# Gate products of a gated linear recurrence: three rounded-fp32 products of high and low halves in place of plain fp32

## The chip, the cores and the metric

The kernel runs on one core of one Trainium2 chip. The metric is the device time of one execution in microseconds (us), and of several executions the median. The core has five engines that work side by side, each with a queue of its own: TensorE (PE) multiplies matrices, VectorE (DVE) and GpSimd (POOL) do elementwise work, ScalarE (ACT) does functions of one input, and SyncE (SP) issues transfers.

## What is computed

One step of a decoder layer for a prompt of 2048 tokens and 8 single tokens of other sequences, all in fp32. After an RMSNorm one combined projection gives five parts. Two of them feed a gated linear recurrence (RG-LRU) of width 512, three feed an attention over a sliding window of 128 tokens. Both results are normalised, put side by side, projected back, and a feed-forward part (SwiGLU, 1024 to 2816 to 1024) follows. The change concerns the two gates of the recurrence, `r` and `i`:

```python
xc, new_conv = _causal_conv(xr, conv_buf, conv_w, conv_b)      # width 4
xb = xc.reshape(xc.shape[:-1] + (8, 64))                       # 8 blocks of 64
r = sigmoid(einsum('btni,nij->btnj', xb, gate_a_w) + gate_a_b)
i = sigmoid(einsum('btni,nij->btnj', xb, gate_x_w) + gate_x_b)
log_a = -8.0 * r * softplus(-lru_lambda)
a = exp(log_a)
u = sqrt(-expm1(2.0 * log_a)) * (i * xc)
h = scan(h * a + u)                                            # over the tokens
rec = h * gelu(gr)
```

## The kernel before

Channels lie on the 128 partitions and tokens on the columns. The 2056 tokens are cut into four sub-blocks: sub-block 0 has 520 columns (the 8 single tokens are its last 8) and is multiplied as two pieces of 260; sub-blocks 1 to 3 have 512. For each of them the input projection runs as 14 units of 128 output channels (`ip<s>_<u>` in the order of matmuls, `ip` in the profile), then come the recurrence, the attention (`s`, `pt`, `o`), and the output projection (`op`). Tokens of all sub-blocks then go through the feed-forward part, which fills the time from 679 us on.

A product of two fp32 matrices is made of rounded fp32 (F32R): each operand is split into a high half, its rounding, and a low half, what the rounding left; `mm3` (L423) issues high times high, high times low and low times high into one accumulator. Weights are split on the way in: `split_raw` has ScalarE round 128x512 values (L368) and GpSimd subtract (L369), and in `w_in0_3_1` the names mean unit 3, second half of the rows, first sub-block (later sub-blocks load the split weights back).

The recurrence runs in `rec_chunk(s, c)` (L768) for each sub-block `s` and each chunk `c` of 128 of the 512 channels: 16 times. GpSimd keeps the last three columns of the chunk in `hist`; the convolution makes `xc` by one operation of ScalarE (L781) and three of VectorE (L786); then come the gates, for each of which a block-diagonal 128x128 matrix is multiplied with `xc` in **plain fp32** (L796 to L802): one matmul per piece of columns, so 4 in sub-block 0 and 2 in the others per chunk, 40 in all (16 of 260 columns, 24 of 512). Their names are `g<s>_<c>_<gate>_<first column>`. ScalarE takes the tanh of each straight from PSUM into `ra` or `ia` (L802). The gate weights stand in one tile `gw`, 128x1024, that SyncE loads in `prologue` (L624).

Order: TensorE's is written out by hand in `PE_ORDER` (L112) up to the start of the feed-forward part; a key with `:n` stands for the next n matmuls of that name, and a key that begins with `w_` for fillers that multiply ones while something else is awaited (`filled`, L311). `order_pe` (L414) chains them, so that a matmul that waits holds all behind it. The other engines' order is chosen when the program is built: a scheduler simulates the engines and takes the ready instruction of the best priority; priorities are due times that the generators of the stages (`Chains`, L234) yield, and `AFTER` (L106) pins seven pairs. So a new instruction on one engine can change the order on all of them. The gate products take turns in one PSUM tile (`ps_m`, one buffer) with other short ones.

```python
for gi, (dst, hb) in enumerate(((ra, hab), (ia, hxb))):
    for n0, nn in nbl:
        ps = m_tile(f"g{s}_{c}_{gi}_{n0}")
        with ahead():
            mm(f"g{s}_{c}_{gi}_{n0}", ps[:, :nn], gw[:, (gi * 4 + c) * P:(gi * 4 + c + 1) * P], xc[:, n0:n0 + nn],
                             start=True, stop=True)
        nc.scalar.activation(dst[:, n0:n0 + nn], ps[:, :nn], AF.Tanh, bias=hb[:, c:c + 1], scale=0.5)
```

Of the kernel before, what the change touches and what calls it, by code (L numbers as in the profile page):

```python
# [117 lines left out]
ip0_8_1:4 bc_x0_4 ip0_8_1:20 ip0_0_0:24 ip0_0_1:23 g0_1_0_0 ip0_0_1 ip0_3_0:24 g0_1_0_260 ip0_3_1:17 g0_1_1_0  # L118
ip0_3_1:7 ip0_11_0:18 g0_1_1_260 ip0_11_0:6 ip0_11_1:15 vt0_0 ip0_11_1:9 ip0_10_0:23 vt0_1 ip0_10_0 ip0_10_1:24
ip0_13_0:10 vt0_2 ip0_13_0:14 ip0_13_1:6 vt0_3 ip0_13_1:18 ip0_2_0:7 s0_0_0:4 ip0_2_0:5 g0_0_0_0 s0_0_1:4 ip0_2_0:12  # L120
ip0_2_1:6 s0_1_0:4 s0_1_1:4 ip0_2_1:2 g0_0_0_260 ip0_2_1:13 pt0_0_1:4 ip0_2_1 s1_0_0:4 ip0_2_1:2 ip0_5_0:3 s1_0_1:4
ip0_5_0 g0_0_1_0 ip0_5_0:9 o0_0_0 ip0_5_0:11 ip0_5_1 s1_1_0:4 ip0_5_1:2 pt0_1_1:4 o0_0_0 ip0_5_1:4 g0_0_1_260
ip0_5_1:12 s1_1_1:2 o0_1_0 s1_1_1:2 ip0_5_1:5 ip0_4_0:6 s2_0_0:4 ip0_4_0:3 o0_1_0 ip0_4_0:11 pt1_0_0:4 ip0_4_0:2
s2_0_1:4 ip0_4_0:2 ip0_4_1:24 ip1_8_0:15 ip0_6_0:2 o1_0_0 ip0_6_0:8 pt1_0_1 o1_0_0 pt1_0_1:3 ip0_6_0 ip1_8_0
g0_3_0_0 ip0_6_0:13 ip0_6_1 ip1_8_0:2 ip0_6_1:15 o1_0_1 g0_3_0_260 s2_1_0:4 ip0_6_1 ip1_8_0 ip0_6_1 pt1_1_0
ip0_6_1:5 o1_0_1 s2_1_1:4 pt1_1_0:3 ip0_6_1 ip1_8_0:5 ip1_9_0 g0_3_1_0 ip1_9_0:19 ip0_7_0:9 ip1_9_0:2 pt1_1_1 o1_1_0
pt1_1_1:3 g0_3_1_260 ip1_9_0:2 ip0_7_0:2 o1_1_0 ip0_7_0:13 w_bc_x1_0 bc_x1_0 s3_0_0:3 s3_0_1:4 ip0_7_1 s3_0_0
ip0_7_1 o1_1_1:2 bc_x1_0 w_pt2_0_0:4 ip0_7_1 bc_x1_0 ip0_7_1 bc_x1_0 ip0_7_1:2 pt2_0_0:4 ip0_7_1:18 ip1_10_0:2
o2_0_0:2 pt2_0_1:3 g0_2_0_0 ip1_10_0:12 pt2_0_1 ip1_10_0:10 ip1_11_0:2 o2_0_1 ip1_11_0 s3_1_0:4 pt2_1_0:4 g0_2_0_260
# [158 lines left out]
def hybrid_step(tc, xT, xR, vecs, cst, gatew, win, wout, wgate, wup, wdown, kT, vC, ck, cv, sconv, sh0,  # L288
# [4 lines left out]
    with ExitStack() as ctx:  # L293
# [291 lines left out]
        with ExitStack() as actx:  # L585
# [3 lines left out]
            ap2 = A(tc.tile_pool(name="ap2", bufs=2))  # L589
            ap3 = A(tc.tile_pool(name="ap3", bufs=2))  # L590

            gw = ap1.tile([P, 1024], F32, name="gw")
            hist = ap1.tile([P, CR, 3], F32, name="hist")
            nc.vector.memset(hist, 0.0)
            carry = ap1.tile([P, CR], F32, name="carry")
# [1134 lines left out]
```

## Time and profile before

| | us |
|---|---|
| median of 3 runs | 2060.22 |
| lowest and highest | 2058.54, 2064.38 |
| the profiled execution: its span | 2054.6 |
| the profiled execution: its own time | not given apart from the span |

One execution was taken by the hardware profiler. Its span is the time from the first to the last instruction of the engines; "busy" is the sum of the records of an engine. A group row names the line, the engine, the operation, the result and its operands, then shapes and types, the count, and behind the bar busy us, mean ns of one, and the idle time of the engine just ahead of these instructions with what ended it. A row of the timeline has the start in us, the duration in us, engine, line, operation, operands and the count of instructions joined, and in brackets the idle time ahead of it and what ended that. A stretch has its bounds and length, the busy time of TensorE's matmuls, of its weight loads, of VectorE, ScalarE and GpSimd with their counts, the granted clock of TensorE, and the share and rate of the transfers. The engine PEld is the weight load, which overlaps the matmuls. A matmul's record reaches to the modelled end of its pipeline, so records of neighbours overlap. L396 is the line of the helper through which all matmuls pass; one plain fp32 matmul leaves two records.

### The profile page before, as it was taken

How to read it: one execution, taken by the hardware profiler on the slowest of the kernel's cores; microseconds unless marked ns; L12 is line 12 of the kernel's file. 1: busy time of each engine (PE TensorE's matmuls, PEld its weight loads, DVE VectorE, ACT ScalarE, POOL GpSimd, SP SyncE). 2: the span in 40 equal slices, each digit the busy share in tenths (PEclk: the TensorE clock that was granted, in tenths of full speed). 3: DMA queues.
4: the chain of work that ended last, by engine and by line, in shares of the span. 5: the costliest groups of instructions: out<-in, count | busy, mean ns of one | idle time of the engine just before them, and what ended most of it. 6: DMA issues, size and time to landing. Idle time of an engine off the chain costs nothing.

```text
span 2054.6 us, 34857 instructions
## 1 busy us (share of the span) xinstructions
PE 2015.9 (98%) x12319; PEld 1908.1 (93%) x12319; DVE 1459.9 (71%) x2694; ACT 944.6 (46%) x1960; POOL 906.5 (44%) x799
## 2 busy tenths in 40 slices
PE   9999999999999999999999999999999999999998
PEld 9988787878777899999999999999999999999998
DVE  6877886767985766666654667777768666777675
ACT  6764774553664543343334533333335433433343
POOL 5311342020122787567656645556457522322333
PEclk9999999999999999999999999999999999999999
DMA  9864584576688856666546677776677675566652
GB/s 329 293 213 143 188 275 159 175 233 210 208 261 280 314 200 223 205 210 207 207 172 210 229 260 258 227 229 221 222 253 265 211 251 189 183 197 196 197 179 96
DMA packets 208991, 450.98 MB, mean 219 GB/s; under 512 B 25232, under 2 KB 82720, under 8 KB 208800
## 3 DMA queue, kind: packets, MB, share of 16 engines
q1 hardware_dynamic: 205184, 445.73, 65.2%
q10 hardware_dynamic: 3632, 3.02, 0.4%
q8 instruction: 97, 1.59, 0.3%
q14 instruction: 78, 0.64, 0.1%
HBM read 335.89 MB, written 113.84 MB: 219 GB/s over the span
## 4 chain that ended last, share of the span: by engine, by line
PE 77%; DVE 9%; DMA 6%; ACT 3%; issue 2%; POOL 1%; SPq 0%; DVEq 0%; ACTq 0%; POOLq 0%
PE ps_u L396 19%; PE ps_g L396 19%; PE pw L396 11%; PE pd L396 10%; PE ip L396 10%; PE op L396 4%; DMA n<-hs 3%; DMA xs<-in_xT 1%; DMA m<-mixed 1%; PE o L396 1%; PE pt L401 1%; DVE sc L974 1%; DVE sc L963 1%; PE s L396 1%; DMA mixed<-n 1%
## 5 line engine op out<-in xcount | busy, mean ns | idle before, releaser
L396 PE MATMUL ps_g<-hn,w_g 128*128 128x342 f32 (+1 forms) x2772 | 489.4, 320 | 4.6 <-DVE c_u L1410 1.8
L396 PE MATMUL ps_u<-hn,w_u 128*128 128x342 f32 (+1 forms) x2772 | 479.9, 319 | 1.9 <-ACT c_u L1436 1.3
L396 PEld LDWEIGHTS ps_g<-hn,w_g 128*128 128x128 f32 x2772 | 445.1, 188 | 6.0 <-DVE c_u L1410 2.3
L396 PEld LDWEIGHTS ps_u<-hn,w_u 128*128 128x128 f32 x2772 | 444.2, 188 | 2.6 <-ACT c_u L1436 1.6
L396 PE MATMUL ip<-xn,w_in 128*128 128x512 f32 (+1 forms) x1680 | 353.4, 358 | 1.9 <-ACT xn L431 1.8
L396 PEld LDWEIGHTS ip<-xn,w_in 128*128 128x128 f32 x1680 | 270.1, 189 | 46.0 <-issue 3.8
L1500 DVE TENSOR_TENSOR y<-y,pw 128x342 f32<-128x342 f32 x504 | 238.7, 504 | 73.0 <-PE pw L396 72.2
L396 PE MATMUL pd<-fh,w_d 128*128 128x344 f32 (+1 forms) x960 | 239.4, 320 | 0.6 <-DVE y L1469 0.6
L396 PE MATMUL op<-mix,w_out 128*128 128x512 f32 (+1 forms) x960 | 203.4, 357 | 0.5 <-DVE rrec L763 0.3
L396 PEld LDWEIGHTS op<-mix,w_out 128*128 128x128 f32 x960 | 155.4, 188 | 29.3 <-issue 5.0
L1469 DVE TENSOR_TENSOR y<-y,pd 128x344 f32<-128x344 f32 (+1 forms) x240 | 117.9, 507 | 75.3 <-PE pd L396 70.7
L396 PEld LDWEIGHTS pd<-fh,w_d 128*128 128x128 f32 x960 | 168.3, 188 | 1.4 <-DVE y L1469 1.1
L396 PE MATMUL pw<-fh,wd 128*128 128x342 f32 x576 | 165.6, 319 | 1.2 <-DVE y L1500 1.2
L396 PE MATMUL pd<-fl,w_d 128*128 128x344 f32 (+1 forms) x480 | 153.4, 320 | 0.0
L1381 DVE TENSOR_TENSOR fl<-c_u,fh 128x342 fp32r<-128x342 f32 (+1 forms) x132 | 107.1, 815 | 48.3 <-ACT fh L1380 47.9
L1225 POOL TENSOR_TENSOR w_u<-ru,w_u 128x512 fp32r<-128x512 f32 x44 | 58.9, 1338 | 181.6 <-ACT w_u L1224 155.0
L1392 POOL TENSOR_TENSOR c_u<-c_u,c_g 128x342 f32<-128x342 f32 (+1 forms) x60 | 60.5, 1008 | 170.7 <-DVE c_u L1410 132.1
L1380 ACT CAST fh<-c_u 128x342 fp32r<-128x342 f32 (+1 forms) x132 | 63.0, 480 | 157.8 <-POOL c_u L1392 61.9
L396 PE MATMUL pw<-t,wd 128*128 128x342 f32 x648 | 126.7, 320 | 2.6 <-DVE t L1381 1.7
L1410 DVE TENSOR_TENSOR c_u<-c_u,ps_u 128x342 f32<-128x342 f32 (+1 forms) x99 | 50.2, 507 | 100.3 <-PE ps_u L396 100.1
L396 PEld LDWEIGHTS pw<-t,wd 128*128 128x128 f32 x648 | 106.0, 188 | 4.4 <-DVE t L1381 2.5
L396 PEld LDWEIGHTS pw<-fh,wd 128*128 128x128 f32 x576 | 105.3, 189 | 1.7 <-DVE y L1500 1.5
(316 smaller groups left out, 3507.4 us busy)
## 6 DMA issues: line engine op xcount, KB each, us to landing
w_g<-split_g SPq DMA_DIRECT2D x88, 512.0 KB, 4.2
w_u<-split_u SPq DMA_DIRECT2D x88, 512.0 KB, 4.9
w_in<-split_w SPq DMA_DIRECT2D x84, 512.0 KB, 3.5
rg<-in_wgate SPq DMA_DIRECT2D x110, 256.0 KB, 3.1
ru<-in_wup SPq DMA_DIRECT2D x110, 256.0 KB, 3.2
w_out<-split_w SPq DMA_DIRECT2D x48, 512.0 KB, 4.4
split_g<-w_g SPq DMA_DIRECT2D x44, 512.0 KB, 3.6
split_u<-w_u SPq DMA_DIRECT2D x44, 512.0 KB, 2.7
```

The source lines that it names most:

```text
L396: r = nc.tensor.matmul(*args, **kw)
L401: r = nc.tensor.transpose(*args)
L963: seen[f"sm{gb}_{kv}_{g}"] = nc.vector.tensor_tensor_reduce(sc[:, g, :kn], ps[:, gi * 256:gi * 256 + kn], mask[:, k0:k0 + kn], -SCALE, ns[ ...
L974: nc.vector.tensor_scalar(sc[:, g, :kn], sc[:, g, :kn], mx[:, 1, g:g + 1], None, ALU.mult)
L1225: lo_eng.tensor_tensor(w[:, 1, :], src, w[:, 0, :].bitcast(F32), op=ALU.subtract)
L1380: nc.scalar.copy(hi, v)
L1381: nc.vector.tensor_tensor(lo, v, hi.bitcast(F32), ALU.subtract)
L1392: (nc.vector if p == NPAIR - 1 or src is not v else eng(E_MUL[2 * h + n])).tensor_tensor(v, src, g, op=ALU.mult)
L1410: nc.vector.tensor_tensor(o, a, b, op)
L1469: r = nc.vector.tensor_tensor(ys[gi, n, m], ys[gi, n, m], ps, ALU.add)
L1500: nc.vector.tensor_tensor(v, v, ps, ALU.add)
```

## The change

The gate weights become two rounded tiles: the raw weights are loaded into a buffer of the pool `bigp`, ScalarE rounds them into `gwh`, GpSimd subtracts into `gwl`. Per chunk two new tiles of one buffer each, `xch` and `xcl` (128x520), are filled in the same way from `xc`. Each gate product becomes three rounded ones, `gwh` with `xch`, `gwl` with `xch`, `gwh` with `xcl`: 120 matmuls for 40. In `PE_ORDER` each `g` key has `:3`, and some stand some matmuls later than before. The scratch for dynamic DMA is set to 2 KB when the program object is made.

```diff
-ip0_8_1:4 bc_x0_4 ip0_8_1:20 ip0_0_0:24 ip0_0_1:23 g0_1_0_0 ip0_0_1 ip0_3_0:24 g0_1_0_260 ip0_3_1:17 g0_1_1_0
+ip0_8_1:4 bc_x0_4 ip0_8_1:20 ip0_0_0:24 ip0_0_1:23 ip0_0_1 ip0_3_0:15 g0_1_0_0:3 ip0_3_0:9 g0_1_0_260:3 ip0_3_1:17
...
-            gw = ap1.tile([P, 1024], F32, name="gw")
+            gwh = ap1.tile([P, 1024], F32R, name="gwh")
+            gwl = ap1.tile([P, 1024], F32R, name="gwl")
...
-                keep(nc.sync.dma_start(gw, gatew))
+                raw = bigp.tile([P, 2 * TM], F32, tag="big", name="graw")[:, :1024]
+                keep(nc.sync.dma_start(raw, gatew))
+                nc.scalar.copy(gwh, raw)
+                nc.gpsimd.tensor_tensor(gwl, raw, gwh.bitcast(F32), op=ALU.subtract)
                 keep(nc.sync.dma_start(sh, sh0))
...
+                xh = ap1.tile([P, TM], F32R, tag="xch", name=f"xch{s}_{c}")
+                xl = ap1.tile([P, TM], F32R, tag="xcl", name=f"xcl{s}_{c}")
+                nc.scalar.copy(xh[:, :T], xc[:, :T])
+                nc.gpsimd.tensor_tensor(xl[:, :T], xc[:, :T], xh[:, :T].bitcast(F32), op=ALU.subtract)
                 yield (t + D_REC[0], "prologue")
...
                         ps = m_tile(f"g{s}_{c}_{gi}_{n0}")
+                        cols = slice((gi * 4 + c) * P, (gi * 4 + c + 1) * P)
                         with ahead():
-                            mm(f"g{s}_{c}_{gi}_{n0}", ps[:, :nn], gw[:, (gi * 4 + c) * P:(gi * 4 + c + 1) * P], xc[:, n0:n0 + nn],
-                                             start=True, stop=True)
+                            for i, (w, x) in enumerate(((gwh, xh), (gwl, xh), (gwh, xl))):
+                                mm(f"g{s}_{c}_{gi}_{n0}", ps[:, :nn], w[:, cols], x[:, n0:n0 + nn], start=i == 0, stop=i == 2)
...
-    nc = bacc.Bacc("TRN2", target_bir_lowering=False, num_devices=1)
+    nc = bacc.Bacc("TRN2", target_bir_lowering=False, num_devices=1, dynamic_dma_scratch_size=2048)
```

What the rows below show is an engine's instructions in the order in which it runs them: line, operation, result and operands (each name with a running number behind it), shape, and how many alike. On GpSimd, early in sub-block 0, where the weights of units 0, 3 and 11 are split and the chunk 1 of the recurrence has its `xc`, this stood before:

```order
L369 TENSOR_TENSOR w_in0_0_1_514<-raw_in0_0_1_512,w_in0_0_1_514 128x512
L902 COPY kvn_152<-kraw0_153 128x8
L369 TENSOR_TENSOR w_in0_3_0_596<-raw_in0_3_0_594,w_in0_3_0_596 128x512
L369 TENSOR_TENSOR w_in0_3_1_602<-raw_in0_3_1_600,w_in0_3_1_602 128x512
L773 COPY xr0_3_592<-hist_133 128x3
L777 COPY hist_133<-xr0_0_504 128x3
L369 TENSOR_TENSOR w_in0_11_0_690<-raw_in0_11_0_688,w_in0_11_0_690 128x512
```

and this stands there now:

```order
L369 TENSOR_TENSOR w_in0_0_1_522<-raw_in0_0_1_520,w_in0_0_1_522 128x512
L931 COPY kvn_153<-vraw0_155 128x8
L911 COPY kvn_153<-kraw0_154 128x8
L369 TENSOR_TENSOR w_in0_3_0_612<-raw_in0_3_0_610,w_in0_3_0_612 128x512
L800 TENSOR_TENSOR xcl0_1_445<-xc0_1_435,xch0_1_444 128x520
L777 COPY xr0_3_608<-hist_134 128x3
L369 TENSOR_TENSOR w_in0_3_1_618<-raw_in0_3_1_616,w_in0_3_1_618 128x512
L781 COPY hist_134<-xr0_0_512 128x3
L369 TENSOR_TENSOR w_in0_11_0_706<-raw_in0_11_0_704,w_in0_11_0_706 128x512
```

The new subtraction of `xcl0_1` and the copy into `xr0_3` have come ahead of the second half of the weights of unit 3, and the order of `hist` and `kvn` has changed. On ScalarE, during the output projection of sub-block 0 (`xt3_1` and `xt3_2` are sums for the norm over loaded rows of sub-block 3, `pth5_1_1` is the rounded transposed probabilities of attention block 5), this stood before:

```order
L741 ACTIVATE xt3_0_4179,xsums3_161<-xt3_0_4179 128x512
L802 ACTIVATE ia1_2_2990<-g1_2_1_0_2999,hxb_150 128x512
L814 ACTIVATE q21_1_3005<-a1_2_3004 128x512
L368 CAST w_out0_6_0_3449<-raw_out0_6_0_3447 128x512
L442 ACTIVATE sq_h0_3_3435<-xres0_3_3237 128x520
L781 ACTIVATE xc1_3_3036<-xr1_3_2828,vec_99 128x512
L741 ACTIVATE xt3_2_4368,xsums3_161<-xt3_2_4368 128x512
L984 CAST pth5_1_1_2457<-pt5_1_1_2452 128x512
L741 ACTIVATE xt3_1_4262,xsums3_161<-xt3_1_4262 128x512
L970 ACTIVATE sc6_1_2511,mx6_1_2512<-sc6_1_2511,mx6_1_2512 128x257 x2
```

and this stands there now:

```order
L368 CAST w_out0_5_1_3460<-raw_out0_5_1_3458 128x512
L811 ACTIVATE ia1_2_3062<-g1_2_1_0_3073,hxb_151 128x512
L368 CAST w_out0_6_0_3533<-raw_out0_6_0_3531 128x512
L745 ACTIVATE xt3_0_4279,xsums3_162<-xt3_0_4279 128x512
L785 ACTIVATE xc1_3_3112<-xr1_3_2892,vec_99 128x512
L442 ACTIVATE sq_h0_3_3519<-xres0_3_3321 128x520
L993 CAST pth5_1_1_2513<-pt5_1_1_2508 128x512
L745 ACTIVATE xt3_1_4366,xsums3_162<-xt3_1_4366 128x512
L979 ACTIVATE sc6_1_2567,mx6_1_2568<-sc6_1_2567,mx6_1_2568 128x257 x2
```

`pth5_1_1` has come ahead of `xt3_2`, which now stands behind these rows. On TensorE, a little ahead of that place (chunk 2 of sub-block 1; the product with `ones` is a filler), this stood before:

```order
L396 MATMUL op0_3_0_3312<-mix0_0_2229,w_out0_3_0_3227 128x260
L396 MATMUL g1_2_0_0_2991<-ones_102 128x256 x5
L396 MATMUL g1_2_0_0_2991<-xc1_2_2885,gw_132 128x512
L401 MATMUL pt5_1_0_2443<-cs_101,sc5_1_2417 128x128
L396 MATMUL op0_3_0_3312<-mix0_0_2229,w_out0_3_0_3227 128x260 x2
L396 MATMUL op0_3_0_3312<-mix0_1_2237,w_out0_3_0_3227 128x260 x3
L396 MATMUL op0_3_0_3312<-mix0_2_2241,w_out0_3_0_3227 128x260 x3
L396 MATMUL op0_3_0_3312<-mix0_3_2603,w_out0_3_0_3227 128x260 x3
```

and this stands there now:

```order
L396 MATMUL op0_3_0_3396<-mix0_0_2285,w_out0_3_0_3311 128x260
L396 MATMUL g1_2_0_0_3063<-ones_102 128x256 x5
L401 MATMUL pt5_1_0_2499<-cs_101,sc5_1_2473 128x128
L396 MATMUL op0_3_0_3396<-mix0_0_2285,w_out0_3_0_3311 128x260 x2
L396 MATMUL op0_3_0_3396<-mix0_1_2293,w_out0_3_0_3311 128x260 x3
L396 MATMUL op0_3_0_3396<-mix0_2_2297,w_out0_3_0_3311 128x260 x2
L396 MATMUL g1_2_0_0_3063<-xch1_2_2958,gwh_132 128x512
L396 MATMUL g1_2_0_0_3063<-xch1_2_2958,gwl_133 128x512
L396 MATMUL g1_2_0_0_3063<-xcl1_2_2959,gwh_132 128x512
L396 MATMUL op0_3_0_3396<-mix0_2_2297,w_out0_3_0_3311 128x260
```

The gate product has moved behind the transposition `pt5_1_0` and seven matmuls of `op0_3_0`; the five fillers have kept their place.

130 lines of the change are left out of this document (65 added, 65 removed).

## The prediction

> **What bounds the kernel now.** I read the page's first part, then the groups of TensorE by shape, then the stretches of 20 us, and last the rows in order of time around the gate products.
>
> ```profile
> span 2054.6 us, 34857 instructions
> PE 2015.9 (98%) x12319; PEld 1908.1 (93%) x12319; DVE 1459.9 (71%) x2694; ACT 944.6 (46%) x1960; POOL 906.5 (44%) x799
> ```
>
> TensorE is busy for all but 38.7 us of the span, so a microsecond taken from its queue is a microsecond of the end, unless another engine then arrives last. The shown runs have a median of 2060.22 us; the profile gives no separate time for its own execution, so I take 5.6 us (2060.2 - 2054.6) as what lies around the span, and every difference below is added to 2060.2.
>
> All gate products lie ahead of 590 us, and in that part there are places where the vector side has no room left (first the tile view of the gate weights, with shortest, median and longest record in ns; then the stretches):
>
> ```profile
> L396 PE MATMUL g<-xc,gw x80: 380/591/697, 40.2 to 589.3; 128*128 128x512 f32 x48, 128*128 128x260 f32 x32
> ...
> 240.00:260.00 20.00, 19.05 (x139) 17.18 (x139) 17.73 (x34) 18.21 (x33) 9.60 (x9) 1.00 0.84 280
> 260.00:280.00 20.00, 16.59 (x125) 15.20 (x124) 18.89 (x32) 16.36 (x37) 12.56 (x12) 1.00 0.93 307
> 480.00:500.00 20.00, 20.00 (x98) 16.27 (x97) 11.12 (x25) 5.23 (x14) 0.19 (x1) 1.00 0.73 235
> 540.00:560.00 20.00, 19.89 (x91) 15.43 (x89) 19.62 (x44) 14.94 (x29) 0.93 (x3) 1.00 0.67 208
> 560.00:580.00 20.00, 19.02 (x86) 14.96 (x87) 19.35 (x38) 13.38 (x26) 3.27 (x4) 1.00 0.77 241
> ```
>
> Columns of a stretch: its bounds, length, busy PE, PEld, DVE, ACT, POOL, granted clock, DMA share, GB/s. At 480 to 500 DVE has 8.9 us free and TensorE alone sets the pace. At 260 to 280 and 540 to 580 DVE is 94 to 98% busy: there a shorter TensorE queue only waits longer.
>
> **TensorE's part.** The tempting rows are the groups:
>
> ```profile
> L396 PE MATMUL g<-xc,gw 128*128 128x512 f32 x48 | 25.1, 605 | 2.5 <-ACT ra L802 2.0 <-DVE xc L786 0.3 <-ACT rb_rc L470 0.2
> L396 PE MATMUL g<-xc,gw 128*128 128x260 f32 x32 | 9.8, 388 | 0.0
> L396 PE MATMUL ip<-xn,w_in 128*128 128x512 f32 x1008 | 263.2, 403 | 0.0
> L396 PE MATMUL ip<-xn,w_in 128*128 128x260 f32 x672 | 92.1, 289 | 1.9 <-ACT xn L431 1.8
> ```
>
> Each plain fp32 product is two records (48 for 24 products of 512 columns, 32 for 16 of 260). By busy time a 512-column product costs 25.1/24 = 1.05 us and three rounded ones 3 x 263.2/1008 = 0.78 us; that would save 24 x 0.26 + 16 x 0.20 = 9.5 us. But busy time counts the pipeline's tail, which the next matmul covers. What the queue pays is from start to start:
>
> ```profile
> 46.20 0.60 PE L396 MATMUL g<-xc,gw 128*128 128x260 f32 x2
> 46.45 3.35 PE L396 MATMUL ip<-xn,w_in 128*128 128x260 f32 x25
> 49.63 0.60 PE L396 MATMUL g<-xc,gw 128*128 128x260 f32 x2
> 49.88 2.87 PE L396 MATMUL ip<-xn,w_in 128*128 128x260 f32 x21
> 52.58 0.27 PE L401 MATMUL vt<-cs,vraw 128*128 128x128 f32 x1
> ...
> 581.77 2.94 PE L396 MATMUL op<-mix,w_out 128*128 128x512 f32 x12
> 584.54 1.02 PE L396 MATMUL g<-xc,gw 128*128 128x512 f32 x2
> 585.00 1.96 PE L396 MATMUL op<-mix,w_out 128*128 128x512 f32 x6
> 586.80 0.39 PE L396 MATMUL o<-pth,vt 128*128 128x512 f32 x1
> ```
>
> Two stretches of one fp32 product and 25 or 21 rounded ones of 260 columns last 3.43 and 2.95 us: four rounded ones make the 0.48 us between them, 0.12 each, and the fp32 product is 3.43 - 25 x 0.12 = 0.43. For 512 columns twelve rounded ones take 2.77 us, 0.231 each; g and six of them take 2.26, so g is 0.875. Three rounded products are 0.36 and 0.69. **Saved: 16 x 0.07 + 24 x 0.18 = 5.4 us**; ends of the range: 5.0 (each of the 40 products 0.01 us less, as far as these rows can be read), and 9.5 if the tail were all uncovered.
>
> [...]
>
> **What is added.** Per chunk and sub-block (16 times) ScalarE rounds `xc` into `xch`, GpSimd subtracts, and the third product waits for `xcl`. The nearest operations, same shape and types, are the weight split's:
>
> ```profile
> L368 ACT CAST w_in<-raw_in 128x512 fp32r<-128x512 f32 x28 | 17.1, 612 | 3.7 <-DMA raw_in<-in_win 2.0 <-POOL hist L777 1.1 <-issue 0.6
> L369 POOL TENSOR_TENSOR w_in<-raw_in,w_in 128x512 fp32r<-128x512 f32 x28 | 38.9, 1392 | 36.3 <-ACT w_in L368 29.3 <-DMA xt<-in_xR 3.0 <-DMA split_w<-w_in 2.9
> ```
>
> So 16 x 0.61 + 1.2 (`gwh`, twice as wide) = 11.0 us on ScalarE and 16 x 1.39 + 2.8 (`gwl`) = 25.0 us on GpSimd, and a delay of about 2.1 us from `xc` to the last product. The gate products that stood less than that behind `xc` are moved back by 3 to 16 matmuls (3 of 512 columns are 0.7 us, 16 of 260 are 1.9), which covers the delay. Two places cost something. At the first, in GpSimd's queue `xcl0_1` now stands ahead of the second half of `w_in0_3`, which had been ready early.
>
> ```profile
> 36.04 4.00 PEld L396 LDWEIGHTS ip<-xn,w_in 128*128 128x128 f32 x33 [0.27 <-POOL w_in L369]
> 36.80 2.79 POOL L369 TENSOR_TENSOR w_in<-raw_in,w_in 128x512 fp32r<-128x512 f32 x2 [0.21 <-ACT w_in L368]
> 38.46 1.68 DVE L786 SCALAR_TENSOR_TENSOR xc<-xr,vec,xc 128x520 f32<-128x520 f32 x1
> 40.20 0.30 PEld L396 LDWEIGHTS g<-xc,gw 128*128 128x128 f32 x2 [0.16 <-DVE xc L786]
> ```
>
> That half was done at 36.80 + 2.79 = 39.6 us. Now the chain is: last operation of `xc0_1`, round (0.6), `xcl0_1` (1.4), a small copy (0.2), the half (1.4), 3.6 us in all. `xc0_1` was done at 40.1, beside that very subtraction; without it by my estimate 1.1 us sooner (the price below), at 39.0. So the half comes at 42.6, or at 43.7 if `xc0_1` is no sooner. TensorE reaches it twelve matmuls of 0.12 after 40.0, near 41.4, and waits 1.2 or 2.3 us, less the two waits in these rows (0.43), which go. I take **+0.6** (0 to +1.9).
>
> The other place is chunk 2 of sub-block 1:
>
> ```profile
> 253.63 1.13 PE L396 MATMUL g<-xc,gw 128*128 128x512 f32 x2 [0.31 <-DVE xc L786]
> 254.99 0.30 PE L401 MATMUL pt<-cs,sc 128*128 128x128 f32 x1 [0.23 <-DVE mx L972]
> ```
>
> Before, the fp32 product ran while TensorE had nothing else until `mx` came. Now the three products stand seven `op` matmuls behind `pt`, where their 0.69 us is no longer hidden: **+0.7** (0 to +0.7). `xcl` would be there at 253.6 + 0.6 + 1.4 = 255.6, the third product's turn is after 255.0 + 7 x 0.12 + 0.46 = 256.3: no wait on top.
>
> A GpSimd subtraction and a DVE operation with two inputs from SBUF do not run side by side:
>
> ```profile
> 33.61 0.75 DVE L786 SCALAR_TENSOR_TENSOR xc<-xr,vec,xc 128x512 f32<-128x512 f32 x1 [0.31 <-POOL kvn L922]
> 34.69 1.85 DVE L786 SCALAR_TENSOR_TENSOR xc<-xr,vec,xc 128x512 f32<-128x512 f32 x1
> 34.70 1.29 POOL L369 TENSOR_TENSOR w_in<-raw_in,w_in 128x512 fp32r<-128x512 f32 x1 [1.14 <-ACT w_in L368]
> ```
>
> The same DVE operation takes 0.75 us alone and 1.85 beside a subtraction. Where DVE has room this hides (480 to 500). Six new subtractions fall where it has little: two chunks of sub-block 1 (250 to 280) and four of sub-block 3 (505 to 590). At 1.85 - 0.75 = 1.10 us each they cost 0 to 6.6 us; some meet DVE operations that read PSUM or DVE's own waits, and I take a third, **+2.0**. In the same stretches TensorE's saving (12 products x 0.18 = 2.2) may be waited away; I give back half, **+1.1**.
>
> [...]
>
> **A stall that moves.** ScalarE's order changes between 260 and 275 us.
>
> ```profile
> 271.97 0.63 ACT L741 ACTIVATE xt<-xt 128x512 f32<-128x512 f32 x1 [2.49 <-DMA xt<-in_xR]
> 272.60 0.57 ACT L984 CAST pth<-pt 128x512 fp32r<-128x512 f32 x1
> 273.22 0.50 PE L396 MATMUL o<-pth,vt 128*128 128x512 f32 x1 [2.09 <-ACT pth L984]
> ```
>
> Before, `xt3_2`, which waits for its load, stands ahead of `pth5_1_1`, and TensorE waits 2.09 us for it. Now `pth5_1_1` comes ahead of `xt3_1` and `xt3_2`. What is late next is DVE's `ptl5_1_1` (DVE was 94% busy), so I count half: **-1.0** (0 to -2.1). A wait at the next place may grow instead: `xch1_3` comes late on a busy ScalarE, but its product has 4 us.
>
> The 2 KB scratch I count at nothing: nearly all data goes through the first of these queues, and no row of before shows a transfer that this scratch holds.
>
> ```profile
> q1 hardware_dynamic: 205184, 445.73, 65.2%
> q10 hardware_dynamic: 3632, 3.02, 0.4%
> ```
>
> If it mattered, loads would land later on all queues at once; I keep that for the tail above the range.
>
> **Sum:** -5.4 + 0.6 + 0.7 + 2.0 + 1.1 - 1.0 = -2.0 us, so **2058.2 us**. From about 760 us on, in the feed-forward part, all five engines' orders are as before; its start is only shifted.
>
> **Rivals.** (1) *Nothing is given back*: DVE follows TensorE's earlier products, and the 2.09 us go whole: -5.4 - 2.1 = -7.5, 2052.7. For it: 480 to 500 shows DVE idle for 44%, and the groups' idle before gates is small; against it: 540 to 580. (2) *The groups' busy time is the price*: -9.5, 2050.7. Against it are the start-to-start rows; only at the few gates that already wait is the tail paid. [...] (4) *No change*: the crowded stretches pull everything back to DVE's pace, so the whole 5.4 is waited away, and a third of the hold-ups less the moved stall remains: +2.0 - 1.0, 2061.2.
>
> **How the numbers follow.** Forecast 0.50 (its own range 2054 to 2061: by the bounds of the hold-ups and of the stall), rival 1 0.22, rival 2 0.05, rival 3 0.13, rival 4 0.10. A measurement of this kernel can tell about 0.3% from no change, 6.2 us: below 2054.0 lie rivals 2 and 1 (0.27) less what spreads up from rival 1, and the forecast's lower end, 0.26 together; above 2066.4 half of rival 3, 0.07; between them 0.67. The range 2051 to 2066 leaves out half of rival 2, part of rival 1, half of rival 3 and the tails, under 2 in 10.
>
> **What would show it.** Right: the gates' group has 120 records, each about as long as an `ip` record (403 and 289 ns), and from the first record of a gate to the next other matmul some 0.69 or 0.36 us; TensorE's wait for `pth` at 273 us is gone or under 1 us; its busy time falls by 5 to 10 us while its idle time grows by some 2 us, mostly at 240 to 280 and 540 to 630. Wrong: waits of `g` for `xcl` over 0.5 us at several places; DVE's operations near the 16 new subtractions at 1.5 to 1.9 us with TensorE idle right after (rival 3); a wait of `ip` for the split of `w_in` near 41 us over 2.3 us; or a later start of the feed-forward part by loads that no row of before shows late.

## The result and the profile after

| | median us (lowest to highest, runs) | against before, 95% interval |
|---|---|---|
| before | 2061.78 (2058.54 to 2064.38, 4) | |
| after | 2082.22 (2079.35 to 2083.13, 4) | 1.0092, 1.0075 to 1.0110 |

The changed kernel is about 19 us slower (0.0092 x 2062); 2058.2 had been forecast, 2051 to 2066 given as the range. The profiled execution of after took 2083.13 us with a span of 2081.3, so 1.8 us lie around the span. The forecast had 5.6 there: the profiled execution of before was one of its shortest, some 5 us under its median, and differences between the two spans (26.7 us) are that much too large. They come in the feed-forward part, which takes 1375.7 us in before, 1378.5 in a run with the same order on VectorE, GpSimd, TensorE and SyncE (scratch_only, below), and 1384.6 in after. Up to the start of that part two executions of one order differ too: by 0.9 us between before and scratch_only, but by up to 4 us near 630 us between after and the run fillers_at_pth (below). Differences of a profile under some 2 us therefore prove little.

The first part of the page of after (span, then busy us, share and instructions of each engine):

```profile
span 2081.3 us, 34977 instructions
PE 2022.3 (97%) x12359; PEld 1921.7 (92%) x12359; DVE 1474.1 (71%) x2694; ACT 953.6 (46%) x1977; POOL 932.2 (45%) x816
```

TensorE is idle for 59.0 us where it was 38.7, and it is busy for 6.4 us more although its queue became shorter. VectorE has the same 2694 instructions, and they take 14.2 us more. Of these, 5.8 us stand in one operation of the prologue that is held up (shown below), and 8.1 us in the operations that run beside the 16 subtractions `xcl`, measured against the median of their like in before and in cast_only (below): about 0.5 us for each.

The groups of the gate products of 512 columns in after, by shape:

```profile
L396 PE MATMUL g<-xcl,gwh 128*128 128x512 f32 x24 | 10.1, 422 | 1.8 <-POOL xcl L800 1.8
L396 PE MATMUL g<-xch,gwh 128*128 128x512 f32 x24 | 10.0, 416 | 4.7 <-ACT ra L811 2.9 <-ACT xch L799 1.6 <-ACT rb_rc L470 0.2
L396 PE MATMUL g<-xch,gwl 128*128 128x512 f32 x24 | 9.5, 395 | 0.0
```

In the timeline of TensorE, from the first record of a gate to the next other matmul (start, duration):

```profile
46.12 0.29 PE L396 MATMUL g<-xch,gwh 128*128 128x260 f32 x1
...
46.48 1.24 PE L396 MATMUL ip<-xn,w_in 128*128 128x260 f32 x9
...
573.77 0.39 PE L396 MATMUL g<-xch,gwh 128*128 128x512 f32 x1
...
574.46 1.79 PE L396 MATMUL op<-mix,w_out 128*128 128x512 f32 x7
```

That is 0.36 and 0.69 us, as forecast: **the 5.4 us of TensorE's queue are saved**. They are lost elsewhere. Two rows say how much has been lost by the start of the feed-forward part, the tile view of its first product `ps_g` (shortest, median, longest ns, then first and last start), of before:

```profile
L396 PE MATMUL ps_g<-hn,w_g x2772: 312/319/424, 678.9 to 2005.7; 128*128 128x342 f32 x132, 128*128 128x344 f32 x66
```

and of after:

```profile
L396 PE MATMUL ps_g<-hn,w_g x2772: 312/319/528, 696.8 to 2032.3; 128*128 128x342 f32 x132, 128*128 128x344 f32 x66
```

The part starts 17.9 us late. Where the delay grows can be read from VectorE, whose instructions are the same in both kernels: paired with before's (the k-th of a name with the k-th), they stand late by these medians:

| us of before | 20-60 | 250-280 | 280-300 | 300-400 | 400-500 | 500-560 | 560-580 | 580-610 | 610-640 | 690-720 | 740-800 |
|---|---|---|---|---|---|---|---|---|---|---|---|
| late by, us | 3.2 | 4.2 | 7.1 | 7.1 | 5.8 | 7.2 | 8.1 | 10.1 | 17.8 | 20.3 | 20.6 |

Four steps: before 60, near 280, near 580, and the largest near 610 (near 630 in the time of after). At or shortly ahead of each the timeline of TensorE in after has a wait (in brackets: its length, and what ended it), and there is a fifth one at 90:

```profile
33.42 0.75 PE L396 MATMUL ip<-xn,w_in 128*128 128x260 f32 x4 [2.21 <-DVE xr L767]
...
90.22 0.50 PE L396 MATMUL o<-pth,vt 128*128 128x512 f32 x1 [2.66 <-DVE ratt L1006]
...
261.48 0.50 PE L396 MATMUL g<-xch,gwh 128*128 128x512 f32 x1 [1.59 <-ACT xch L799]
...
263.38 0.79 PE L396 MATMUL g<-xcl,gwh 128*128 128x512 f32 x1 [1.16 <-POOL xcl L800]
...
580.23 0.50 PE L396 MATMUL g<-xch,gwh 128*128 128x512 f32 x1 [2.12 <-ACT ra L811]
...
633.88 0.80 PE L396 MATMUL o<-pth,vt 128*128 128x512 f32 x1 [5.97 <-ACT pth L993]
```

**Most of these waits cost more than their length**, because TensorE's clock fell afterwards. The stretches of after around the waits of 33, 580, 634 and 90 us (columns as in the stretches of the prediction; the granted clock is the third number from the end):

```profile
31.30:34.71 3.41, 1.28 (x10) 1.29 (x11) 2.93 (x12) 0.30 (x2) 0.66 (x1) 1.00 0.90 233
34.72:38.13 3.41, 3.41 (x18) 3.41 (x17) 2.18 (x4) 1.86 (x4) 2.06 (x3) 0.50 1.03 394
...
577.43:580.84 3.41, 1.29 (x8) 0.95 (x8) 3.41 (x7) 3.40 (x12) 0.00 (x0) 1.00 0.13 52
580.85:584.26 3.41, 3.41 (x14) 2.94 (x13) 2.89 (x6) 3.41 (x7) 1.03 (x1) 0.50 0.61 171
...
632.05:635.46 3.41, 1.58 (x4) 1.29 (x5) 2.61 (x10) 2.23 (x5) 1.28 (x1) 0.50 0.96 328
635.46:638.88 3.42, 3.42 (x12) 2.85 (x11) 1.87 (x7) 2.20 (x9) 0.00 (x0) 0.50 0.62 221
...
85.92:89.33 3.41, 1.64 (x14) 1.43 (x12) 3.41 (x11) 2.42 (x7) 0.00 (x0) 1.00 0.98 348
89.34:92.74 3.40, 2.52 (x20) 2.48 (x21) 3.18 (x9) 1.89 (x4) 0.00 (x0) 1.00 0.61 202
```

The bounds lie on one grid of 3.413 us (from 34.72 to 580.85 are 160 of them, from there to 632.05 are 15). A window in which TensorE works for 1.3 or 1.6 us is followed by one at 0.50, in which it does about half the work (in after the products of `op` of 512 columns start 0.43 us apart at 0.50 and 0.23 at 1.00): up to 1.7 us are lost. In the window from 31.30 TensorE was idle for 2.1 us (3.41 - 1.28). The last pair holds the wait of 2.66 us, which a bound of the grid cut in two; the clock stayed at 1.00. Ahead of 760 us before has one window at half clock (from 210.83 us), in which half of TensorE's busy time is 1.45 us. After has eight (from 7.42, 34.72, 215.63, 263.42, 580.85, 632.05, 635.46 and 717.39 us), in which it is 12.7 us: +11.3 us. With them the first 760 us can be added up: TensorE's waits of 0.25 us or more are 20.7 us in all in before and 37.5 in after, +16.8; +11.3 by the clock; -5.4 saved; together **+22.7**, beside 20.6 in the table. The sum is 2 us too large, and no better than that.

How little work brings the half clock can be read from the traces of all 17 kernels, from 24 to 756 us, window by window on the grid. Behind a window at full clock that holds under 1.5 us of TensorE's records the next was at half clock in all 48 cases; with 1.5 to 2.0 us it was in 13 of 49, and with more in 2 of 3473.

### The profile page after: what moved, and what is told of

It reads as the page before. It is cut to its first block, busy times and chain, and to the rows that moved or that the text cites. A ratio compares the mean times of both kernels' runs of the same rounds, so it can differ in the third digit from the quotient of the medians.

```text
span 2081.3 us, 34977 instructions
## 1 busy us (share of the span) xinstructions
PE 2022.3 (97%) x12359; PEld 1921.7 (92%) x12359; DVE 1474.1 (71%) x2694; ACT 953.6 (46%) x1977; POOL 932.2 (45%) x816
## 3 DMA queue, kind: packets, MB, share of 16 engines
q8 instruction: 97, 1.59, 0.3%
## 4 chain that ended last, share of the span: by engine, by line
PE 71%; DVE 11%; DMA 9%; ACT 4%; issue 3%; POOL 1%; SPq 1%; DVEq 0%; ACTq 0%; POOLq 0%
PE ps_u L396 19%; PE ps_g L396 18%; PE pd L396 10%; PE pw L396 9%; PE ip L396 8%; DMA n<-hs 3%; PE op L396 2%; DMA xt<-in_xR 1%; DMA mixed<-n 1%; DVE n L521 1%; DVE y L1509 1%; DVE sc L972 1%; DVE xn L432 1%; PE s L396 1%; PE o L396 1%
```

## The experiments

Ratios are to runs of before on the same chip; 0.001 is 2.1 us. The experiments of one heading below did not always run together, so they are compared by their ratios. "Start" is the first `ps_g`, 678.9 us in before and 696.8 in after.

### The parts added to the kernel before

The scratch alone:

```diff
-    nc = bacc.Bacc("TRN2", target_bir_lowering=False, num_devices=1)
+    nc = bacc.Bacc("TRN2", target_bir_lowering=False, num_devices=1, dynamic_dma_scratch_size=2048)
```

> The kernel before with nothing but the 2 KB scratch for dynamic DMA; the order of every engine is that of before. Theory (the loss comes from waits of TensorE that the new operations and the new orders make, and from the half clock behind them): no change, 2059 to 2064 us. Rival (the smaller scratch makes the transfers slower, and everything behind them late): most of the 20 us, 2075 to 2083.

2058.67 us, 1.0007 (0.9996 to 1.0019), start 678.0. The scratch costs nothing that can be measured, as forecast.

The vector side alone, with the fp32 products:

```diff
+                nc.scalar.copy(xh[:, :T], xc[:, :T])
+                nc.gpsimd.tensor_tensor(xl[:, :T], xc[:, :T], xh[:, :T].bitcast(F32), op=ALU.subtract)
```

> The kernel before with the 2 KB scratch and, in each of the 16 chunks, the rounding into xch and the subtraction into xcl, whose results nobody reads; the gate products stay plain fp32 from xc, TensorE's order is that of before. Theory (the added operations cost little by themselves; the loss sits in the prologue's weight split, in products that wait for xcl, and in the later place of the feed-forward part's loads, none of which is here): 2062 to 2070 us. Rival (GpSimd's subtractions hold VectorE up everywhere): without TensorE's saving of 5.4 us it is no faster than after, 2082 to 2090.

2064.75 us, 1.0031 (1.0018 to 1.0044): +6.4 us, though nobody waits for either tile. Start 681.4. With the new operations the scheduler also chose other orders (ScalarE's differs from 37 us on, SyncE's from 59, VectorE's from 67), so this is the price of both. Two kernels take it apart: the first of these lines alone,

> The kernel before with the small scratch and the sixteen casts xch on ScalarE alone; no subtraction, and nobody reads xch. vector_side_only, which also had the sixteen subtractions on GpSimd, measured 1.0031. If the subtractions hold VectorE up (theory: about 16 x 0.8 us of VectorE time in the profile of after), this kernel stands near before: ratio 1.0000 to 1.0010. Rival: the casts, which stand in ScalarE's queue ahead of the exponentials, are what costs: ratio about 1.003.

and both, with `nc.vector` in place of `nc.gpsimd`:

> vector_side_only with the sixteen subtractions on VectorE instead of GpSimd; still nobody reads them. Theory: a subtraction on GpSimd takes about 0.8 us of VectorE's time by holding it up, and on VectorE about 0.7 us as work, so that the ratio is that of vector_side_only, 1.002 to 1.0045, with VectorE's busy time 8 to 12 us above before's. Rival: the hold-ups fall into idle time of VectorE and the cost of vector_side_only is GpSimd's own queue; then this kernel is faster, 1.0000 to 1.0015.

cast_only 2063.94 us, 1.0017 (1.0005 to 1.0028), start 682.1; low_on_vector 2066.07 us, 1.0039 (1.0025 to 1.0053), start 687.5. The busy rows of cast_only:

```profile
PE 2019.8 (98%) x12319; PEld 1911.4 (93%) x12319; DVE 1455.4 (71%) x2694; ACT 953.4 (46%) x1976; POOL 904.3 (44%) x799
```

of vector_side_only:

```profile
PE 2017.6 (98%) x12319; PEld 1908.7 (93%) x12319; DVE 1465.5 (71%) x2694; ACT 953.5 (46%) x1976; POOL 930.7 (45%) x815
```

and of low_on_vector:

```profile
PE 2020.1 (98%) x12319; PEld 1910.3 (93%) x12319; DVE 1467.2 (71%) x2710; ACT 954.3 (46%) x1976; POOL 907.2 (44%) x799
```

Beside cast_only VectorE's busy time grows by 10.1 us when GpSimd subtracts and by 11.8 when VectorE does it itself. But the same 2694 instructions take 1455.4 us in cast_only and 1459.9 in before, so beside before it grows by 5.6 and 7.3. Taken one by one, the operations beside the 16 subtractions of vector_side_only are 7.2 us longer than the median of their like, 0.45 us for each; a subtraction on VectorE takes 0.69 us (median). So on GpSimd it saves VectorE little. What that costs in time is less clear.

The kernel with the casts alone costs some 3.5 us, which had been forecast at nothing. In its profile they come at one place (timelines of ScalarE and TensorE in cast_only):

```profile
104.74 0.63 ACT L741 ACTIVATE xt<-xt 128x512 f32<-128x512 f32 x1 [3.50 <-DMA xt<-in_xR]
...
107.30 1.24 PE L396 MATMUL g<-xc,gw 128*128 128x260 f32 x2 [2.71 <-ACT ra L804]
```

The tanh `ra` stands behind `xt`, whose load comes late (the wait for it is 0.29 us in before), TensorE waits for the tanh, a half-clock window follows at 107.23, and VectorE's delay goes from 0.8 us to 4.6 and is still 3.2 us at 620 to 640. So the 3.5 us are not shown to be the time of the casts; they came with an order in which this load is late. The step from 1.0017 to 1.0031 lies within the intervals, and the starts (682.1 and 681.4) show none. So the hold-ups alone are worth 0 to about 6 us, and how the 6.4 are shared out stays open.

The third part, after's order of TensorE, with fp32 products (one of the moved places; `:3` left away in all):

```diff
-w_g1_2_0_0:5 g1_2_0_0 pt5_1_0 op0_3_0:12
+w_g1_2_0_0:5 pt5_1_0 op0_3_0:7 g1_2_0_0 op0_3_0:5
```

> The kernel before, plain fp32 gate products and nothing added, but each gate product at the place in TensorE's order that it has after the change. Theory (the moves by 3 to 16 matmuls cost little by themselves: at most the 0.7 us at chunk 2 of sub-block 1 and a later tanh at 570): ratio to before 0.999 to 1.0015. Rival (the later places make the recurrence late, and that makes the losses after 500 us): ratio 1.003 or more.

2066.85 us, 1.0016 (1.0002 to 1.0030): +3.3 us, start 684.8. Moving the products back costs something without any new operation; the interval nearly reaches 1, and the scheduler's other orders (SyncE's differs from 49 us on, VectorE's from 57) are in the price.

### The wait for `pth` near 634

In after ScalarE's timeline shows `pth` behind a cast that waits for a load of the feed-forward part's stage (`hn` comes from the mixed states `m`):

```profile
632.34 0.48 ACT L577 CAST hn<-m 128x344 fp32r<-128x344 f32 x1 [3.76 <-DMA m<-mixed]
...
633.26 0.57 ACT L993 CAST pth<-pt 128x512 fp32r<-128x512 f32 x1
```

First theory: ScalarE's order. Four such casts are pinned behind `pth14_1_1`:

```diff
+    ("hh0_1_0", "pth14_1_1"), ("hh0_1_1", "pth14_1_1"), ("hh0_1_2", "pth14_1_1"), ("hh0_1_3", "pth14_1_1"),
```

> The changed kernel with ScalarE's first four roundings of the loaded m (rows of product 1) pinned behind pth14_1_1, for which TensorE waited 5.97 us at 634. Theory (that wait was made by ScalarE's order: roundings that wait for late loads stand ahead of pth14_1_1): the wait is under 1 us, the two half-clock windows at 632 to 639 go, and 6 to 9 us are gained: 2073 to 2077 us. Rival (the loads are late anyway, and the wait moves on to the next pth or to the start of the feed-forward part): 2080 to 2084.

2079.5 us, 1.0099 (1.0079 to 1.0120): nothing gained. TensorE's wait moved on (timeline of casts_behind_pth):

```profile
637.44 0.58 PE L397 MATMUL bc_rc<-ones 128*128 128x256 f32 x1 [7.36 <-DVE rccols L454]
```

Now VectorE stood behind its own operation on a late `m`. The theory fell: not the order on ScalarE, the load itself is late. Does the clock matter there? Fifty fillers (products of ones, in after 0.12 us from start to start at full clock) keep TensorE at work while it waits:

```diff
-op2_7_0:6 o14_1_1 op2_7_0:8
+op2_7_0:6 w_st_rc3:50 o14_1_1 op2_7_0:8
```

> [...] Theory (a window of 3.41 us in which TensorE stood idle is followed by one at half clock): pth comes no earlier, but the clock stays at 1.00 from 632 to 639, which gains 0.5 x 6.8 = 3.4 us at most: 2078 to 2081 us. Rival (the half clock has another cause, or the end hangs on the loads and not on TensorE): 2082 to 2084.

2074.24 us, 1.0074 (1.0055 to 1.0094), start 691.8: 3.7 us by the ratios, 5.0 by the start, and the intervals overlap. The profile does not let the clock have this gain. ScalarE's timeline of fillers_at_pth has the awaited cast at

```profile
629.00 0.56 ACT L993 CAST pth<-pt 128x512 fp32r<-128x512 f32 x1
```

4.3 us ahead of after, where it starts at 633.26. The first load of `m` is issued at 617.2 in place of 621.0, ahead of the first filler (623.61), although VectorE, GpSimd and SyncE run in after's order. So "pth comes no earlier" did not hold, and 4.3 of the 5.0 us have nothing to do with the clock; why this execution was ahead no run shows. One half-clock window is left here (from 634.99; half of its busy time is 1.6 us) of after's two (2.5 us together), so by these traces the clock is worth about 0.9 us at this place.

Why is the load late? SyncE's queue issues it. The tile view of `m` (first and last start of its 28 loads) in before:

```profile
L576 SPq DMA_DIRECT2D m<-mixed x28: 319/327/1086, 599.9 to 691.5; - x28
```

and in after:

```profile
L576 SPq DMA_DIRECT2D m<-mixed x28: 319/341/1532, 621.0 to 711.3; - x28
```

The first load is issued 21.1 us later, while VectorE at that point is some 10 to 18 us late. Ahead of it the same queue carries the mixing's loads `n<-hs` and stores `mixed<-n`, each of which waits for the one before it through VectorE; between them stand the weight loads `w_in` and `w_out`, which wait until a buffer is free. From 518 us of before on, transfers of the mixing slip behind weight loads, by one at first and later by up to three. The first slip, SyncE's timeline of before:

```profile
517.68 0.87 SPq L525 DMA_DIRECT2D mixed<-n  x2
518.65 0.40 SPq L380 DMA_DIRECT2D w_in<-split_w  x1
```

and of after:

```profile
524.48 0.32 SPq L525 DMA_DIRECT2D mixed<-n  x1
524.89 0.38 SPq L380 DMA_DIRECT2D w_in<-split_w  x1
526.41 0.32 SPq L525 DMA_DIRECT2D mixed<-n  x1
```

Their lag grows along the queue: the 5th load `n` is 5.8 us late (498.8 to 504.6 us), the 11th 8.3, the 17th 15.1, the 21st 20.8 (575.4 to 596.2). The next kernel is after with 109 transfers of SyncE chained in before's order:

```diff
+        def order_sp():
+            seq = SP_ORDER.split()
+            for a, b in zip(seq, seq[1:]):
+                behind(seen[b], seen[a])
```

> The changed kernel with one thing put back: SyncE's queue keeps, from the first load of the feed-forward mixing n0_0_1 to the load m0_2_1, the order that it had before among those loads and stores and the weight loads (109 transfers chained); TensorE's order is untouched. Theory (after the change each of these small transfers stands one to three weight loads later in SyncE's queue, which wait for a buffer; the chain of 24 round trips slips from 6 to 21 us behind, and TensorE waits for it at 634): the chain slips by no more than the rest of the kernel, the wait of 6 us and its two half-clock windows go, and 8 to 12 us are gained: ratio to before 1.0035 to 1.0055 (after: 1.0092). Rival (the queue's order follows from VectorE being late; put back, the weight loads wait for it instead): TensorE waits for weights in 520 to 600, ratio 1.008 to 1.011.

2074.59 us, 1.0050 (1.0033 to 1.0066), against 1.0092 (1.0075 to 1.0110): the intervals do not meet. **The order of SyncE's queue cost 8.7 us by the ratios**, 6.5 by the start (690.3). From 530 us on the scheduler also places some operations of VectorE and GpSimd elsewhere than in after, which is in the price. The step near 610 is gone: VectorE is 10.8 us behind before at 580 to 610 us and 11.2 at 610 to 640. In sp_order the tile view of `m` has

```profile
L601 SPq DMA_DIRECT2D m<-mixed x28: 319/326/909, 609.8 to 705.1; - x28
```

and the wait of 5.97 us is

```profile
628.74 0.50 PE L408 MATMUL o<-pth,vt 128*128 128x512 f32 x1 [0.26 <-ACT pth L1018]
```

One half-clock window is left there, from 634.12.

### The weights' low half at the start

In after GpSimd's timeline has, one behind the other,

```profile
23.39 1.19 POOL L454 TENSOR_TENSOR xcols<-xcols,nhalf 104x5 f32<-104x5 f32 x1 [0.17 <-DVE xcols L453]
24.54 2.40 POOL L628 TENSOR_TENSOR gwl<-graw,gwh 128x1024 fp32r<-128x1024 f32 x1
26.90 2.52 POOL L369 TENSOR_TENSOR w_in<-raw_in,w_in 128x512 fp32r<-128x512 f32 x2
```

and VectorE's, in that time,

```profile
23.49 5.95 DVE L642 TENSOR_TENSOR sp<-sp 128x4 f32<-128x4 f32 x1
29.47 0.17 DVE L643 TENSOR_TENSOR sp<-sp 128x4 f32<-128x4 f32 x1
```

An operation on four columns, whose like takes 0.17 us in the next row, is held from 23.5 to 29.4, to the end of the third subtraction; the first operation in GpSimd's rows, also with two inputs, ran when it began. What VectorE has to do next, `xr` among it, comes late, and TensorE waits the 2.21 us at 33.42. So `gwl` on VectorE:

```diff
-                nc.gpsimd.tensor_tensor(gwl, raw, gwh.bitcast(F32), op=ALU.subtract)
+                nc.vector.tensor_tensor(gwl, raw, gwh.bitcast(F32), op=ALU.subtract)
```

> The changed kernel with the one subtraction that makes gwl (128x1024) on VectorE in place of GpSimd. Theory (gwl and the two weight splits behind it held one small VectorE operation of the prologue for 5.95 us; the evictions behind it came late, TensorE waited 2.21 us and ran a window of 3.41 us at half clock): the wait at 33 us is under 0.6 us, no half clock follows, and everything up to 240 us is 3 to 4 us earlier; of that 2 to 4 us reach the end: ratio 1.0072 to 1.0085. Rival (the late start is made good by slack at 200 to 280 us): ratio 1.009 to 1.010.

2079.78 us, 1.0080 (1.0061 to 1.0100), start 696.7 as in after: no gain can be shown. The wait at 33 is gone, and another has come (timeline of gwl_on_vector):

```profile
44.67 0.39 PE L396 MATMUL ip<-xn,w_in 128*128 128x260 f32 x1 [2.07 <-POOL w_in L369]
```

This is the wait for `w_in0_3` that the prediction had near 41 us, at 1.2 to 2.3 us. In after the late start hides all but 0.15 us of it.

### Chunk 2 of sub-block 1

ScalarE's timeline of after; `xc` was done at 257.34:

```profile
257.17 0.61 ACT L368 CAST w_out<-raw_out 128x512 fp32r<-128x512 f32 x1
257.79 1.28 ACT L828 ACT_TABLE_LOAD   x1
259.09 1.06 ACT L828 ACTIVATE q<-q 128x1024 f32<-128x1024 f32 x1
260.17 0.61 ACT L952 CAST qst<-qraw 64x512 fp32r<-64x512 f32 x1
260.81 0.62 ACT L799 CAST xch<-xc 128x512 fp32r<-128x512 f32 x1
```

The cast starts 3.5 us behind its input, behind four operations that were in the queue. `xcl` is ready 6.0 us after `xc`, not 2.1. Over the 16 chunks that delay is 2.0 to 6.0 us, 2.95 on average. With the product moved 20 matmuls further back:

```diff
-op0_3_0:7 g1_2_0_0:3 op0_3_0:5 o5_0_1 op0_3_0:2 pt5_1_0:3 op0_3_0:9 op0_3_260:17
+op0_3_0:12 o5_0_1 op0_3_0:2 pt5_1_0:3 op0_3_0:9 g1_2_0_0:3 op0_3_260:17
```

> The changed kernel with the product g1_2_0_0 of chunk 2 in sub-block 1 another 19 matmuls later in TensorE's order (17 of op, 4 of pt in all behind). Theory (the rounding of xc waited 3.5 us in ScalarE's queue and GpSimd came 2.6 us after; TensorE stood 1.59 and 1.16 us for them and then ran a window at half clock): both waits are under 0.4 us, the half clock at 263 to 267 goes, 3 to 4 us are gained there and 2 to 4 at the end: ratio 1.0072 to 1.0085. Rival (the stretch 250 to 300 goes at ScalarE's and VectorE's pace; the waits reappear within 30 us): ratio 1.009 to 1.010.

2077.93 us, 1.0069 (1.0052 to 1.0085), start 693.4: 4.7 us by the ratios, 3.4 by the start; the intervals overlap a little. The two waits for `xch` and `xcl` and the half-clock window at 263 are gone; the chunk's second gate now waits for the first one's tanh, since both use the one PSUM buffer (timeline of chunk2_later):

```profile
268.20 0.50 PE L396 MATMUL g<-xch,gwh 128*128 128x512 f32 x1 [1.61 <-ACT ra L811]
```

A second new wait, of 1.46 us for `xcl`, stands at 286.90. So a part of the two waits came back within 30 us, as the rival had it.

### All together

sp_order, gwl_on_vector and chunk2_later in one kernel:

> The three edits together: SyncE's order of before in that segment, gwl on VectorE, g1_2_0_0 later. Theory (the three losses add up and what remains is the change as forecast): ratio 0.999 to 1.003, about 2056 to 2065 us beside a before of 2058 to 2062. Rival (the losses share one cause and do not add): ratio 1.004 or more.

2070.2 us, 1.0036 (1.0023 to 1.0048), start 687.4. The gains do not add in full: 11.5 us of the 15.9 that the three had by their ratios. Two more order edits on top, the second half of `w_in0_3` ahead of `xcl0_1`, and `ra3_2`, for which TensorE waits at 580, ahead of all exponentials but one:

```diff
+    ("ex14_0_1", "ra3_2"), ("ex14_0_2", "ra3_2"), ("ex14_0_3", "ra3_2"),
+    ("xcl0_1", "wl_in0_3_1"), ("hx0_3", "xcl0_1"), ("hi0_0", "xcl0_1"),
+    ("xch0_1", "wh_in0_3_1"),
```

> three_put_back and two more orders put back: on GpSimd and ScalarE the second half of w_in0_3 ahead of xcl0_1 again (it made TensorE wait 2.07 us at 44), on ScalarE the tanh ra3_2 behind one exponential of sc14_0 again in place of three or four (2.19 us at 579). Theory (each of these waits with its half-clock window is worth 2 to 4 us): ratio 1.000 to 1.002 (three_put_back: 1.0036). Rival (what remains is VectorE's time, and the waits come back elsewhere): ratio 1.003 to 1.0045.

2068.1 us, 1.0035 (1.0024 to 1.0047): the same time, though the start is 683.1. Other waits of about 2 us came up (1.72 at 45.58 for `ra`, 2.05 at 236.24 for `rrec`). And these five with the cast `xch` on VectorE, to take it out of ScalarE's queue:

```diff
-                seen[f"xch{s}_{c}"] = nc.scalar.copy(xh[:, :T], xc[:, :T])
+                seen[f"xch{s}_{c}"] = nc.vector.tensor_copy(xh[:, :T], xc[:, :T])
```

> five_put_back with the rounding of xc into xch on VectorE, right behind the operation that makes xc, in place of ScalarE. Theory (the rounding waited 0.7 to 3.5 us in ScalarE's queue in 7 of 16 chunks; VectorE does it in about 0.4 us at once): no wait of TensorE for xch or xcl over 0.3 us at 255 to 290 and 348; 1 to 3 us less than five_put_back. Rival (VectorE is the engine short of time; 16 x 0.4 us more on it is felt): 1 to 4 us more.

2076.57 us, 1.0073 (1.0050 to 1.0096): 7.8 us slower than with the cast on ScalarE (the pin of `xch0_1` behind `w_in0_3`, which was one of ScalarE's, is left out). That VectorE's time is the cause is not shown. TensorE waits four times for weight loads of the chained transfers, 0.76 to 1.25 us at 587 to 612 and then (timeline of five_cast_on_vector)

```profile
626.49 4.78 PE L412 MATMUL op<-mix,w_out 128*128 128x512 f32 x13 [6.92 <-DMA w_out<-split_w]
```

At the last one VectorE's delay behind five_put_back goes from 4.7 to 12.9 us. The chain puts these loads behind transfers of the mixing, so that they come late when VectorE is late.

### What the low half costs where products wait for it

sp_order without `xcl`:

```diff
-                nc.gpsimd.tensor_tensor(xl[:, :T], xc[:, :T], xh[:, :T].bitcast(F32), op=ALU.subtract)
...
-                            for i, (w, x) in enumerate(((gwh, xh), (gwl, xh), (gwh, xl))):
+                            for i, (w, x) in enumerate(((gwh, xh), (gwl, xh), (gwh, xh))):
```

> The kernel sp_order (changed kernel, SyncE's order of before in the mixing) without xcl and its 16 subtractions on GpSimd; the third product multiplies gwh with xch a second time, so TensorE has as many matmuls as after, and the gates lack the low half of xc. Theory (the subtractions hold VectorE's operations up by some 0.8 us each, of which a third is felt, and TensorE waits for xcl at three places): 3 to 7 us less than sp_order (1.005): ratio 1.0015 to 1.0035. [...] Rival (the subtractions are hidden): ratio 1.004 to 1.006.

2064.98 us, 1.0017 (1.0007 to 1.0028), start 681.3: 6.8 us less than sp_order (1.0033 to 1.0066), intervals apart. And sp_order with the subtraction `xcl` on VectorE (`nc.vector` in its line):

> sp_order with the sixteen subtractions xcl on VectorE; the products read them. sp_order measured 1.0050 and the same without the subtractions 1.0017. Theory: VectorE is the engine that is short of time whichever engine subtracts, so 1.004 to 1.006. Rival: the low half's way through GpSimd's queue is the cost, and 1.002 to 1.0035.

2076.0 us, 1.0080 (1.0066 to 1.0093), worse than both theories had it. Two long waits in TensorE's timeline of this kernel say why, one for `xcl`, which stands in VectorE's queue, and one for a weight load of the chained transfers:

```profile
576.39 0.50 PE L408 MATMUL g<-xcl,gwh 128*128 128x512 f32 x1 [4.58 <-DVE xcl L825]
...
624.32 5.01 PE L408 MATMUL op<-mix,w_out 128*128 128x512 f32 x13 [5.57 <-DMA w_out<-split_w]
```

Up to the second one VectorE is ahead of sp_order, by 2.9 us at 600 to 620 us, and from there on 3.7 us behind: the chain again. So this run cannot tell VectorE's lack of time from a single bad place. Unread, the subtractions cost 0 to about 6 us; read, with the hold-ups, 6.8. How much of that is the hold-up of VectorE and how much the wait for `xcl` stays open.

## Why the prediction was wrong

Point by point, by its steps:

- **TensorE's 5.4 us: right.** 0.36 and 0.69 us stand in the rows; the groups' busy time (rival 2) was no price.
- **The scratch at nothing: right** (1.0007).
- **The stall at 273: the move happened, its gain is not shown.** No wait for `pth` stands at that place in after. Since TensorE lost time ahead of it at 258 to 263, no gain can be told apart.
- **`w_in0_3`, +0.6: right mechanism, hidden.** 0.15 us in after, 2.07 where the start was put right. What the sum lacked was `gwl`: it was counted as 2.8 us of GpSimd's time and not as three subtractions in a row that hold VectorE for 6 us while TensorE starts up.
- **Chunk 2, +0.7 and "no wait on top": wrong.** The step that failed is "`xcl` would be there at 253.6 + 0.6 + 1.4": the cast was taken to start when `xc` is done. ScalarE's queue put 3.5 us ahead of it; TensorE waits 1.59 and 1.16 us and then runs a half-clock window. Undone: 3.4 to 4.7 us, with intervals that overlap a little.
- **Hold-ups +2.0 and saving waited away +1.1: too small in all, though one hold-up was priced too high.** An `xcl` lengthens VectorE's records by about 0.5 us, not by the 1.10 that one row had given. But the vector side alone costs 6.4 us, and the kernel with the casts alone, priced at nothing, 3.5 of them, by a load that came late; in the full kernel the low half costs 6.8 us. Rival 3, which counts all six hold-ups at 1.10 us and the saving of their stretches as waited away (6.6 + 2.2; 2066.2 in all), had the bound, but that the hold-ups carry it could not be shown.
- **The moves at nothing but chunk 2: too low by about 2.6 us, if the middle of the interval holds.** moves_alone costs 3.3 (0.4 to 6.2), chunk 2's 0.7 among it.
- **The order of the other engines: the largest error.** The working takes up ScalarE's order near 273 and GpSimd's near 40, and says that from about 760 us on all orders are as before. SyncE's queue, in which the transfers of the mixing slip from about 520 us on, has no term in the sum and no rival: it was put at nothing without a reason. Only the last sentence names a later start of the feed-forward part by loads, as what would make the forecast wrong. The slip cost 8.7 us by the ratios, 6.5 by the start.
- **The size of a wait.** Each was priced at its own length. Where TensorE had stood for some 2 us within one window, up to 1.7 us came on top: 12.7 us in eight windows ahead of 760 us, 1.45 in one window in before.

Of the rivals the third came nearest, with 2066.2; no case reached past it, since none had a queue slip. The parts overlap (three edits that gained 15.9 us one by one gained 11.5 together), so they are not to be summed. What the runs show is that no kernel with the rounded gate products was faster than before: the best, no_low_half, which leaves a subtraction out, is at 1.0017, the best complete one at 1.0035. The whole saving is 0.26% of the time, less than this kernel's measurement can tell, and the order of SyncE's queue alone takes more.

## What to carry to other kernels

Where a scheduler chooses the order, compare the transfer queues as closely as the engines: small dependent transfers that slip behind loads which wait for a buffer lose a little at each step, and the sum appears far away, at an engine that merely stands in line (here 6.5 to 8.7 us at 634 us by an edit of products that end at 600). Price a new operation between two engines by what is already in the queue of the engine that gets it, not by its input's time. Chaining the queue in its old order is no cure for every kernel: with more work on VectorE TensorE waited 5.57 and 6.92 us for loads in the chain. Where TensorE is busy for 98%, a saving in its queue is worth only as much as the other engines can follow (here nothing was left of 5.4 us), and a new wait can cost more than its length (the one of 2.12 us at 580 was followed by a window at half clock, in which up to 1.7 us more were lost).

## What was not expected of the hardware

- In after the half clock came, ahead of 760 us, behind windows in which TensorE was at work for 0 to 1.8 of 3.41 us, always for whole windows of one grid; a wait of 2.66 us across a bound of the grid had no effect. Over all traces, under 1.5 us of work in a window brought it every time (48 of 48), over 2.0 us almost never (2 of 3473).
- An operation of VectorE on four columns was held for 5.95 us by three GpSimd subtractions in a row, although by its record it stood there from 23.49 and the first of them began at 24.54: it was not let in ahead of them or between them.
- A GpSimd subtraction of 128x512 lengthens VectorE's records by about 0.5 us (8.1 us by the 16 of after, 7.2 by those of vector_side_only), not much less than the 0.69 us that VectorE takes to do it.
